# Decoder step on one core: the attention output's inverse norms made once a head instead of once per pair of query blocks

## The chip, the cores and the metric

The kernel runs on one core of one Trainium2 chip. The metric is device microseconds (us) of one execution. Three runs of the kernel before gave 3199.22, 3204.20 and 3204.82 us.

## What is computed

One step of a hybrid decoder layer: a SwiGLU feed-forward half step, a mixer that adds differential attention and retention under two gates, a second feed-forward half step, and a final norm. There is a prompt of 1024 rows and a sample of 8 x 4 rows, so 1056 rows in all. The part that matters here is the differential attention of the prompt (8 heads, each with two score maps of depth 64 and one value of width 128) and what becomes of its output:

```python
s = jnp.einsum('bqhcd,bkhcd->bhcqk', qh, kh)           # two maps c per head
p = jax.nn.softmax(jnp.where(mask, s, NEG_INF), axis=-1)
a = p[:, :, 0] - lam * p[:, :, 1]
o_a = jnp.einsum('bhqk,bkhv->bqhv', a, v)
o_a = rms_norm(o_a, subln_g, SUBLN_EPS) * (1.0 - lam_init)
merged = jax.nn.sigmoid(ga) * o_a + jax.nn.sigmoid(gb) * o_r
x = x + gate2 * (merged @ w_out)
```

The norm is over the 128 values of a head, so each query row of each head has one inverse norm. Keys and values of the prompt are outputs too.

## The kernel before

**Layout.** Activations lie transposed: features on the 128 partitions, rows along the free dimension, in 3 row blocks of 352. A large matrix product is made in three matmuls from a high and a low part of both operands (`mm3`, L228 to L230; `split`, L172 to L179, makes the parts: ACT rounds the high one, DVE or POOL subtracts for the low one).

**Stages.** Feed-forward 1, then the mixer, then feed-forward 2 and the final norm. The stage of this text is the differential attention, about 1480 to 2190 us. Its loop (L1236 to L1244) runs over heads h = 0 to 7 and weaves two generators. The *main* one is the gates' half units of earlier heads (`gates`, L1198) and then the projections of q, k and v of head h+1 (`qkv`, 18 steps); a step is 12 matmuls of 128x352. The *side* one is `attention(h)` (L1082). `weave` takes side steps at the ratio `DST`/(main steps), with `DST` = 52 (L888). So the order of the work is what these generators yield, and the instructions of each engine then run in the order in which they were recorded and scheduled, each waiting by semaphore for what it needs.

**attention(h).** The setup scales and splits q and k (`st`, `kk`, `kl`), turns k and v back into rows by transposes on PE (`kt` L1108, `vt` L1115, two halves of 512 rows each), copies each half from PSUM to SBUF on ACT (`ko` L1110, `vo` L1117; ring `kvo` of `KVO` = 4 buffers, L887) and stores it on POOL's queue (L1111, L1118), and splits v (`vh`, `vl`). Then, in five rounds, `scores(sb)` for the pair sb of query blocks (L1123) stands beside `values(sb-1)` (L1154). `scores` makes both maps of each block (PSUM `s`, L1133, two large buffers in all), mask and maximum on DVE (`mx` L1137), the exponential with row sums on ACT (`P` L1139), the norm's softmax term `l` (L1144) and the combination of both maps on DVE (L1149). `values` transposes the combined maps (`at`, L1163), splits them (`ah`, `al`) and multiplies with the values into `o`.

**The norm at the end of `values`.** ACT squares `o` (`osq` L1175) and copies it with the gain into `on`. Then `rsqrt_g` (L340): two matmuls with a column of ones sum the squares over the partitions (`rqo`, L347), so that each query row has its sum on a partition of its own; `rsqrt_cols` (L315) makes the inverse square root of [128, 2] on DVE by three Newton steps (L323 to L337, column by column for up to two columns); DVE multiplies the identity by each column (`rdo`, L359); after `RY` = 3 empty yields two matmuls ones x diagonal (L364) spread the inverse norms over all partitions. DVE multiplies `on` by them (L1180) and POOL's queue stores 128 KB to `od` in memory (L1181). This happens 4 times a head, 32 times in all.

**gates(h)** (L1198) makes the two gates of a head in row blocks, first g = 0 (the attention's, reads `od` back, L1213, and writes `M`, L1215) and then g = 1 (the retention's, reads `rd` and `ud`, adds to `M` on POOL and stores it to `md`). The gates of head 7 run later, beside w_out.

Of the kernel before, what the change touches and what calls it, by code (L numbers as in the profile page):

```python
# [11 lines left out]
F32 = mybir.dt.float32  # L12
# [3 lines left out]
ALU = mybir.AluOpType  # L16
# [4 lines left out]
P = 128  # L21
D = 1024
KT = 8
SEQ = 1024
# [4 lines left out]
NRB = 3  # L29
# [74 lines left out]
def build(tc, i):  # L104
    nc = tc.nc
    V, S, T, G = nc.vector, nc.scalar, nc.tensor, nc.gpsimd
    ld = nc.sync.dma_start
    st = nc.gpsimd.dma_start
# [29 lines left out]
    def aux_ps(name):  # L138
        return banks[0][1].tile([P, 512], F32, tag="aux", name=name, bufs=banks[0][3])
# [5 lines left out]
    od = [dr.tile([P, SEQ], F32, name=f"od{k}") for k in range(KT)]  # L145
    rd = [dr.tile([P, SEQ], F32, name=f"rd{k}") for k in range(KT)]
# [23 lines left out]
    def acth(out, in_, scale=1.0):  # L170
        if isinstance(scale, float):
            S.activation(out, in_, AF.Copy, scale=scale)  # L172
        else:
            S.activation(out, in_, AF.Identity, scale=scale)
# [97 lines left out]
    with tc.tile_pool(name="init", bufs=1) as ip:  # L272
        vec = ip.tile([P, P], F32, name="vec")
        o = 0
# [40 lines left out]
    def rsqrt_cols(sums, scale, eps, name):  # L315

        m, n = sums.shape
        x, h, a, y = (rsq.tile([P, 4], F32, tag=f"r{c}", name=f"r{c}{name}", bufs=2)[:m, :n] for c in "xhay")
        yi = y.bitcast(I32)
        if isinstance(eps, float):  # L320
            V.tensor_scalar(out=x, in0=sums, scalar1=scale, scalar2=eps, op0=ALU.mult, op1=ALU.add)
        else:
            V.scalar_tensor_tensor(out=x, in0=sums, scalar=scale, in1=eps, op0=ALU.mult, op1=ALU.add)  # L323
# [16 lines left out]

    def rsqrt_g(src, n, scale, eps, name):


        p_ = aux_ps(f"rq{name}")
        blocks = [(c, min(P, n - c)) for c in range(0, n, P)]
        for j, (c, w_) in enumerate(blocks):
            T.matmul(p_[:w_, 500 + j:501 + j], src[:, c:c + w_], ones[:, 0:1], start=True, stop=True)  # L347
        nb, w0 = len(blocks), blocks[-1][1]
        full = nb if w0 == P else nb - 1
        r = []  # L350
        for m, a, b in ((P, 0, full), (w0, full, nb)):
            if b > a:
                e = eps if isinstance(eps, float) else eps[:m, a:b]
                y = rsqrt_cols(p_[:m, 500 + a:500 + b], scale, e, f"{name}_{a}")
                r += [y[:, j:j + 1] for j in range(b - a)]
        dg = []
        for j, (c, w_) in enumerate(blocks):
            d = rsq.tile([P, P], F32, tag="rd", name=f"rd{name}_{j}", bufs=3)
            V.tensor_scalar(out=d[:w_, :w_], in0=ident[:w_, :w_], scalar1=r[j], scalar2=None, op0=ALU.mult)  # L359
            dg.append(d)  # L360
        for _ in range(RY):
            yield
        for j, (c, w_) in enumerate(blocks):
            T.matmul(p_[:, c:c + w_], ones[:w_, :], dg[j][:w_, :w_], start=True, stop=True)  # L364
        return p_
# [521 lines left out]
    KVO = 4  # L887
# [154 lines left out]
    with ExitStack() as left, ExitStack() as right:  # L1042
# [38 lines left out]

        def attention(h):  # L1082
# [40 lines left out]
            def scores(sb, A):  # L1123
                for qb in (2 * sb, 2 * sb + 1):
# [19 lines left out]
                    V.scalar_tensor_tensor(out=l2[sb][:, q:q + 1], in0=rs[:, 0:1], scalar=1e-5, in1=rs[:, 0:1],  # L1144
# [9 lines left out]
            def values(sb, A):  # L1154
# [21 lines left out]
                on = dp.tile([P, 256], F32, tag="on", name=f"on{h}_{sb}", bufs=2)  # L1176
                acth(on[:], po[:, :256], subg[:])
                yield
                rr = yield from rsqrt_g(sq[:], 256, 1.0 / P, l2[sb][:], f"o{h}_{sb}")
                V.tensor_tensor(out=on[:], in0=on[:], in1=rr[:, :256], op=ALU.mult)  # L1180
                st(out=od[h][:, sb * 256:(sb + 1) * 256], in_=on[:])  # L1181

            A = [[] for _ in range(4)]
            l2 = [dp.tile([P, 2], F32, tag="l2", name=f"l2_{h}_{sb}", bufs=4) for sb in range(4)]
            for sb in range(5):
                two = [scores(sb, A[sb])] if sb < 4 else []
                if sb:
                    two.append(values(sb - 1, A[sb - 1]))
                while two:
                    for g in list(two):  # L1190
                        try:
                            next(g)
                        except StopIteration:
                            two.remove(g)
                            continue
                        yield

        def gates(h):  # L1198
            M = gp.tile([P, SEQ], F32, tag="M", name=f"M{h}")
            ws = {}  # L1200
            for g, rb in ([(g, rb) for g in range(2) for rb in range(NRB)] if h < 7 else
                          [(g, rb) for rb in range(NRB) for g in range(2)]):
# [9 lines left out]
                ov = gp.tile([P, RB], F32, tag="gv", name=f"gv{h}_{g}{rb}", bufs=2)  # L1212
                (st if h == 7 else ld)(out=ov[:, :n], in_=(od, rd)[g][h][:, rc])  # L1213
                if g == 0:
                    V.scalar_tensor_tensor(out=M[:, rc], in0=t[:, :n], scalar=1.0, in1=ov[:, :n], op0=ALU.add, op1=ALU.mult)  # L1215
                    if n < RB:
                        V.tensor_scalar(out=gas[:, h, :], in0=t[:, n:], scalar1=1.0, scalar2=None, op0=ALU.add)
                else:
# [3 lines left out]
                    V.scalar_tensor_tensor(out=ov[:, :n], in0=t[:, :n], scalar=1.0, in1=ov[:, :n], op0=ALU.add, op1=ALU.mult)  # L1222
                    G.tensor_tensor(out=M[:, rc], in0=M[:, rc], in1=ov[:, :n], op=ALU.add)
                    st(out=md[h // 2][h % 2 * P:(h % 2 + 1) * P, rc], in_=M[:, rc])
# [182 lines left out]
```

## Time and profile before

| what | value |
|---|---|
| median of 3 runs | 3204.2 us (3199.22 to 3204.82) |
| the profiled execution | 3204.28 us, span 3202.5 us |
| TensorE matmul (PE) busy | 3060.3 us, 96% of the span |
| VectorE (DVE) busy | 1700.5 us, 53% |
| ScalarE (ACT) busy | 1151.3 us, 36% |
| GpSimd (POOL) busy | 452.0 us, 14% |
| granted TensorE clock, mean | 0.986 |
| memory traffic | 254.18 MB, 79 GB/s |

The span runs from the first to the last instruction; 1.8 us of the execution lie around it. PE is the matmuls and PEld the weight loads, which overlap them. Busy times are shares of the whole span and say nothing of one stage; a matmul's end is modelled, so PE's records overlap a little. In the rows, a name is that of a tile in the program without its buffer number, L is a line of the kernel printed above, and "idle before <- X" is how long the engine had stood idle ahead of an instruction and whose work ended that.

### The profile page before, as it was taken

The page shows a single profiled execution, that of the slowest core. Times are in us where ns is not written, and L with a number is a line of the kernel's source. Part 1 is how long each engine was busy: PE and PEld are TensorE (multiplying, and loading weights), DVE is VectorE, ACT ScalarE, POOL GpSimd, SP SyncE. Part 2 cuts the span into 40 slices and gives each one's busy share as a digit, 9 for nine tenths or more (in the row PEclk, how much of TensorE's full clock was granted, in tenths as well). Part 3 has the DMA queues.
Part 4 walks back from the last instruction along what each step waited for, and adds up shares of the span by engine and source line. Part 5 has one row for each costly group of instructions (what it writes and reads, how often), then busy time and mean ns, then how long its engine had stood idle before and what let it go on. Part 6 is the DMA issues. An engine that isn't in the chain of part 4 may idle for free.

```text
span 3202.5 us, 47920 instructions
## 1 busy us (share of the span) xinstructions
PE 3060.3 (96%) x19135; PEld 2925.4 (91%) x19135; DVE 1700.5 (53%) x3683; ACT 1151.3 (36%) x2164; POOL 452.0 (14%) x456
## 2 busy tenths in 40 slices
PE   7999999999999999999999998998999999999998
PEld 4999999999999999988888888988889999999998
DVE  6443434334366666668867777776655323233235
ACT  5422232222234243346555556554444111111113
POOL 2000000000132222212222222223021000000002
PEclk9999999999999999999999999998999999999999
DMA  6232222221131322222221121225622111111111
GB/s 215 61 116 81 80 91 87 86 79 53 52 121 59 100 77 83 89 84 84 75 65 60 56 71 56 73 68 172 202 74 66 47 46 47 47 47 47 47 47 61
DMA packets 261369, 254.18 MB, mean 79 GB/s; under 512 B 13216, under 2 KB 223649, under 8 KB 261146
## 3 DMA queue, kind: packets, MB, share of 16 engines
q1 hardware_dynamic: 245226, 200.38, 20.5%
q0 software_dynamic: 15920, 50.74, 4.5%
q8 instruction: 150, 2.46, 0.3%
q14 instruction: 73, 0.60, 0.1%
HBM read 207.56 MB, written 43.52 MB: 78 GB/s over the span
## 4 chain that ended last, share of the span: by engine, by line
PE 39%; DVE 9%; ACT 3%; issue 1%; DMA 1%; POOL 0%; DVEq 0%; SPq 0%; ACTq 0%; POOLq 0%
PE pb L228 3%; PE pa L228 3%; PE pa L229 3%; PE pa L230 3%; PE pb L229 3%; PE pb L230 3%; PE po L228 3%; PE po L229 2%; PE po L230 2%; PE gp L228 1%; PE gp L230 1%; PE gp L229 1%; ACT P L1139 1%; PE at L1163 1%; DVE rao L334 1%
## 5 line engine op out<-in xcount | busy, mean ns | idle before, releaser
L513 DVE TENSOR_TENSOR silu<-silu,pb 128x352 f32<-128x352 f32 x132 | 68.7, 521 | 503.5 <-PE pb L230 501.4
L172 ACT ACTIVATE gh<-silu 128x352 fp32r<-128x352 f32 x132 | 65.2, 494 | 325.4 <-DVE silu L513 325.2
L484 DVE SCALAR_TENSOR_TENSOR Y<-po,mod,Y 128x352 f32<-128x352 f32 (+1 forms) x144 | 82.1, 571 | 123.3 <-PE po L230 123.2
L447 POOL TENSOR_TENSOR acc<-acc,sq 128x352 f32<-128x352 f32 x27 | 29.8, 1103 | 804.7 <-ACT sq L446 795.8
L484 DVE SCALAR_TENSOR_TENSOR X<-po,mod,X 128x352 f32<-128x352 f32 (+1 forms) x144 | 81.7, 570 | 112.1 <-PE po L230 111.6
L512 ACT ACTIVATE silu<-pa 128x352 f32<-128x352 f32 x132 | 60.5, 458 | 205.9 <-PE pa L230 205.8
L1139 ACT ACTIVATE P<-s,mx 128x256 f32<-128x256 f32 (+7 forms) x128 | 94.9, 742 | 80.4 <-DVE mx L1137 72.2
L447 POOL TENSOR_TENSOR accf<-accf,sq 128x352 f32<-128x352 f32 x9 | 8.8, 974 | 726.8 <-ACT sq L446 726.8
L228 PE MATMUL po<-gh,wo_0h 128*128 128x352 f32 x288 | 94.6, 328 | 5.1 <-DVE X L484 4.1
L1137 DVE TENSOR_REDUCE mx<-s 128x1 f32<-128x256 f32 (+7 forms) x128 | 95.5, 752 | 1.8
L229 PE MATMUL po<-gl,wo_0h 128*128 128x352 f32 x288 | 93.8, 326 | 0.0
L230 PE MATMUL po<-gh,wo_0l 128*128 128x352 f32 x288 | 93.7, 325 | 0.0
L179 DVE TENSOR_TENSOR gl<-silu,gh 128x352 fp32r<-128x352 f32 x132 | 69.1, 524 | 46.2 <-ACT gh L172 45.8
L228 PE MATMUL po<-gh,wo_1h 128*128 128x352 f32 x288 | 93.4, 324 | 0.0
L230 PE MATMUL po<-gh,wo_1l 128*128 128x352 f32 x288 | 92.8, 322 | 0.0
L229 PE MATMUL po<-gl,wo_1h 128*128 128x352 f32 x288 | 92.6, 322 | 0.0
L172 ACT ACTIVATE ah<-at 128x512 fp32r<-128x512 f32 (+1 forms) x80 | 44.4, 555 | 98.4 <-PE at L1163 97.7
L228 PE MATMUL po<-gh,wo_3h 128*128 128x352 f32 x240 | 77.5, 323 | 1.2 <-DVE rs L489 1.2
L228 PE MATMUL po<-gh,wo_2h 128*128 128x352 f32 x240 | 77.7, 324 | 0.0
L229 PE MATMUL po<-gl,wo_2h 128*128 128x352 f32 x240 | 77.2, 322 | 0.0
L229 PE MATMUL po<-gl,wo_3h 128*128 128x352 f32 x240 | 77.2, 322 | 0.0
L230 PE MATMUL po<-gh,wo_2l 128*128 128x352 f32 x240 | 77.2, 321 | 0.0
(1511 smaller groups left out, 11358.7 us busy)
## 6 DMA issues: line engine op xcount, KB each, us to landing
ada_0r<-ada_w SPq DMA_DIRECT2D x18, 512.0 KB
ada_1r<-ada_w SPq DMA_DIRECT2D x18, 512.0 KB
ada_2r<-ada_w SPq DMA_DIRECT2D x18, 512.0 KB
ada_3r<-ada_w SPq DMA_DIRECT2D x18, 512.0 KB
st<-state_ret SPq DMA_DIRECT2D x32, 256.0 KB
state_ret_sample<-st POOLq DMA_DIRECT2D x32, 256.0 KB, 2.3
kp<-cache_k SPq DMA_DIRECT2D x64, 128.0 KB
vp<-cache_v SPq DMA_DIRECT2D x64, 128.0 KB
```

The costliest lines, as they stand in the source:

```text
L172: S.activation(out, in_, AF.Copy, scale=scale)
L179: (eng or V).tensor_tensor(out=l, in0=src, in1=f(h), op=ALU.subtract)
L228: T.matmul(out, wh, xh, start=first and j == 0, stop=False)
L229: T.matmul(out, wh, xl, start=False, stop=False)
L230: behind[0] = T.matmul(out, wl_, xh, start=False, stop=last and j == n - 1).ins
L334: V.scalar_tensor_tensor(out=a[:, j:j + 1], in0=y[:, j:j + 1], scalar=y[:, j:j + 1], in1=h[:, j:j + 1], op0=ALU.mult, op1=ALU.mult)
L447: (V if k % 2 else G).tensor_tensor(out=acc[k % 2], in0=acc[k % 2], in1=sq[:], op=ALU.add)
L484: V.scalar_tensor_tensor(out=x[k][:, c0:c0 + n], in0=p_[:, :n], scalar=gt[:, k, 0:1], in1=x[k][:, c0:c0 + n], op0=ALU.mult, op1=ALU.add)
L512: S.activation(s_[:], pa[:, :RB], AF.Silu)
L513: V.tensor_tensor(out=s_[:], in0=s_[:], in1=pb[:, :RB], op=ALU.mult)
L1137: V.tensor_reduce(out=mx[:], in_=ss[:, :wd], op=ALU.max, axis=AX.X, negate=True)
L1139: S.activation(pt[:, :wd], ss[:, :wd], AF.Exp, bias=mx[:], accum_out=rs[:, c:c + 1])
```

## The change

`rsqrt_g` goes. At the end of `values`, the two sums of a pair are added to the softmax terms in one tile `l2` of 8 columns (one DVE operation), and `on` becomes one tile of 128x1024 for the head (one buffer). A new generator `finish` makes one inverse square root of all 8 columns with `rsqrt_cols` (which for more than two columns goes by whole tiles), yields three times, and then, in two halves, makes four spread matmuls, one multiply of 128x512 and one store of 256 KB. A spread matmul now has the column itself, repeated 128 times, as its stationary operand, and the identity as the moving one; no diagonals are made. `finish` of head h is queued beside the first scores of head h+1 (`ends`); that of head 7 runs at its own end. In `gates` g = 1 now comes first and g = 0 second, and before g = 0 reads `od` it drains what is left of `finish`. `KVO` falls from 4 to 3, and the small tiles of `rsqrt_cols` grow from 4 to 8 columns.

```diff
     def rsqrt_cols(sums, scale, eps, name):
-        x, h, a, y = (rsq.tile([P, 4], F32, tag=f"r{c}", ..., bufs=2)[:m, :n] for c in "xhay")
+        x, h, a, y = (rsq.tile([P, 8], F32, tag=f"r{c}", ..., bufs=2)[:m, :n] for c in "xhay")
-        if isinstance(eps, float):
+        if scale is None:
+            x = sums
+        else:
             V.tensor_scalar(out=x, in0=sums, scalar1=scale, scalar2=eps, op0=ALU.mult, op1=ALU.add)
-        else:
-            V.scalar_tensor_tensor(out=x, in0=sums, scalar=scale, in1=eps, op0=ALU.mult, op1=ALU.add)
...
-    def rsqrt_g(src, n, scale, eps, name):
...
-    KVO = 4
+    KVO = 3
...
+        ends = {}
         def attention(h):
...
-                    V.scalar_tensor_tensor(out=l2[sb][:, q:q + 1], in0=rs[:, 0:1], scalar=1e-5, in1=rs[:, 0:1],
+                    V.scalar_tensor_tensor(out=l2[:, qb:qb + 1], in0=rs[:, 0:1], scalar=1e-5, in1=rs[:, 0:1],
...
-                on = dp.tile([P, 256], F32, tag="on", name=f"on{h}_{sb}", bufs=2)
-                acth(on[:], po[:, :256], subg[:])
+                acth(on[:, sb * 256:(sb + 1) * 256], po[:, :256], subg[:])
                 yield
-                rr = yield from rsqrt_g(sq[:], 256, 1.0 / P, l2[sb][:], f"o{h}_{sb}")
-                V.tensor_tensor(out=on[:], in0=on[:], in1=rr[:, :256], op=ALU.mult)
-                st(out=od[h][:, sb * 256:(sb + 1) * 256], in_=on[:])
+                pq = aux_ps(f"rq{h}_{sb}")
+                for j in range(2):
+                    T.matmul(pq[:, j:j + 1], sq[:, j * P:(j + 1) * P], ones[:, 0:1], start=True, stop=True)
+                V.scalar_tensor_tensor(out=l2[:, 2 * sb:2 * sb + 2], in0=pq[:, :2], scalar=1.0 / P,
+                                       in1=l2[:, 2 * sb:2 * sb + 2], op0=ALU.mult, op1=ALU.add)
+
+            def finish():
+                r = rsqrt_cols(l2[:], None, None, f"o{h}")
+                for _ in range(RY):
+                    yield
+                for hf in range(2):
+                    pr = aux_ps(f"rr{h}_{hf}")
+                    for j in range(4):
+                        T.matmul(pr[:, j * P:(j + 1) * P], r[:, 4 * hf + j:4 * hf + j + 1].to_broadcast([P, P]), ident[:],
+                                 start=True, stop=True)
+                    o_ = on[:, hf * 512:(hf + 1) * 512]
+                    V.tensor_tensor(out=o_, in0=o_, in1=pr[:], op=ALU.mult)
+                    st(out=od[h][:, hf * 512:(hf + 1) * 512], in_=o_)
+                    yield
...
-            l2 = [dp.tile([P, 2], F32, tag="l2", name=f"l2_{h}_{sb}", bufs=4) for sb in range(4)]
+            l2 = dp.tile([P, 8], F32, tag="l2", name=f"l2_{h}", bufs=2)
+            on = dp.tile([P, SEQ], F32, tag="on", name=f"on{h}")
             for sb in range(5):
                 two = [scores(sb, A[sb])] if sb < 4 else []
+                if sb == 0 and h:
+                    two.append(ends[h - 1])
...
+            ends[h] = finish()
+            if h == 7:
+                yield from ends[h]

         def gates(h):
...
-            for g, rb in ([(g, rb) for g in range(2) for rb in range(NRB)] if h < 7 else
-                          [(g, rb) for rb in range(NRB) for g in range(2)]):
+            for g, rb in ([(g, rb) for g in (1, 0) for rb in range(NRB)] if h < 7 else
+                          [(g, rb) for rb in range(NRB) for g in (1, 0)]):
...
+                if g == 0:
+                    for _ in ends[h]:
+                        pass
                 (st if h == 7 else ld)(out=ov[:, :n], in_=(od, rd)[g][h][:, rc])
                 if g == 0:
-                    V.scalar_tensor_tensor(out=M[:, rc], in0=t[:, :n], scalar=1.0, in1=ov[:, :n], op0=ALU.add, op1=ALU.mult)
+                    V.scalar_tensor_tensor(out=ov[:, :n], in0=t[:, :n], scalar=1.0, in1=ov[:, :n], op0=ALU.add, op1=ALU.mult)
+                    G.tensor_tensor(out=M[:, rc], in0=M[:, rc], in1=ov[:, :n], op=ALU.add)
+                    st(out=md[h // 2][h % 2 * P:(h % 2 + 1) * P, rc], in_=M[:, rc])
...
-                    V.scalar_tensor_tensor(out=ov[:, :n], in0=t[:, :n], scalar=1.0, in1=ov[:, :n], op0=ALU.add, op1=ALU.mult)
-                    G.tensor_tensor(out=M[:, rc], in0=M[:, rc], in1=ov[:, :n], op=ALU.add)
-                    st(out=md[h // 2][h % 2 * P:(h % 2 + 1) * P, rc], in_=M[:, rc])
+                    V.scalar_tensor_tensor(out=M[:, rc], in0=t[:, :n], scalar=1.0, in1=ov[:, :n], op0=ALU.add, op1=ALU.mult)
```

**Where the instructions now stand.** The rows below are instructions in the order of their engine; the line numbers of the changed kernel are 23 to 25 lower in this part.

DVE before, the end of head 1: the chain of its pair 2 (`rxo`, `ryo`, `rho`, `rao`), among the combination of the maps (`P`), the splits of head 2's keys (`kk`, `kl`) and the rotation of its queries (`q2t`).

```order
L323 SCALAR_TENSOR_TENSOR rxo_2_0_15196<-rqo_2_15193,l_1_2_14508 128x2
L1147 SCALAR_TENSOR_TENSOR rs_7_15104<-rs_7_15104,nlam 128x1
L324 TENSOR_SCALAR ryo_2_0_15199<-rxo_2_0_15196 128x2
L326 TENSOR_SCALAR rho_2_0_15197<-rxo_2_0_15196 128x2
L1149 SCALAR_TENSOR_TENSOR P_70_15113<-P_71_15158,rs_7_15104,P_70_15113 128x1024
L325 TENSOR_SCALAR ryo_2_0_15199<-ryo_2_0_15199 128x2
L1101 COPY ks<-dak 128x32
L334 SCALAR_TENSOR_TENSOR rao_2_0_15198<-ryo_2_0_15199,rho_2_0_15197 128x1 x2
L337 SCALAR_TENSOR_TENSOR ryo_2_0_15199<-rao_2_0_15198,ryo_2_0_15199 128x1
L1097 CAST kk_2_15494<-kk_2_15494 64x1024
```

DVE of the changed kernel, the end of head 1: the sum of the last pair, the chain on all 8 columns (its other two Newton rounds follow in the same manner), then head 2.

```order
L179 TENSOR_TENSOR al_33_15126<-at_33_15121,ah_33_15125 128x384
L1158 SCALAR_TENSOR_TENSOR l_1_14392<-rq_3_15151,l_1_14392 128x2
L325 TENSOR_SCALAR ryo_15407<-l_1_14392 128x8
L327 TENSOR_SCALAR rho_15405<-l_1_14392 128x8
L326 TENSOR_SCALAR ryo_15407<-ryo_15407 128x8
L330 TENSOR_TENSOR rao_15406<-ryo_15407 128x8
L331 TENSOR_TENSOR rao_15406<-rao_15406,rho_15405 128x8
L332 SCALAR_TENSOR_TENSOR ryo_15407<-rao_15406,ryo_15407 128x8
```

The chain moved from the middle of each round to the head's end, once, and nothing stands between its links.

PE before, the spread of that pair 2 of head 1, among the projection of head 2's queries (`q2p`).

```order
L229 MATMUL q2p_15241<-hl_119,q2h 128x352
L230 MATMUL q2p_15241<-hh_111,q2l 128x352
L228 MATMUL q2p_15241<-hh_112,q2h 128x352
L229 MATMUL q2p_15241<-hl_120,q2h 128x352
L364 MATMUL rqo_2_15193<-rdo_2_0_15216,ones 128x128
L364 MATMUL rqo_2_15193<-rdo_2_1_15218,ones 128x128
L230 MATMUL q2p_15241<-hh_112,q2l 128x352
L228 MATMUL q2p_15241<-hh_113,q2h 128x352
```

PE of the changed kernel, the first spread of head 1, among head 2's scores (`s`) and the gate of an earlier head (`gp`).

```order
L230 MATMUL gp_12_15474<-hh_109,g_1l 128x352
L1110 MATMUL s_11_15487<-kk_2_15297,st_2_15295 128x256
L1111 MATMUL s_11_15487<-kl_2_15299,st_2_15295 128x256
L1169 MATMUL rr_0_15499<-ident,ryo_15407 128x128 x4
L228 MATMUL gp_12_15474<-hh_110,g_1h 128x352
L229 MATMUL gp_12_15474<-hl_118,g_1h 128x352
```

The spread moved out of its own head into the next one, behind the second query block's scores; the second half (`rr_1`) follows 12 gate matmuls later.

ACT before, the setup of head 2, with the semaphores that each instruction waits for (DMASW is the landing of a store on POOL's queue).

```order
L1110 ACTIVATE ko_15519<-kt_15514 128x512 [waits DMASW5_49,PE_49]
L1117 ACTIVATE vo_15527<-vt_15522 128x512 [waits PE_49]
L1120 ACTIVATE vs<-dav 128x32 [waits Activation_49]
L172 ACTIVATE vh_15512<-vo_15527 128x512 [waits Activation_49]
L1110 ACTIVATE ko_15537<-kt_15532 128x512 [waits DMASW0_49,PE_49]
L1117 ACTIVATE vo_15545<-vt_15540 128x512 [waits DMASW1_49,PE_49]
L172 ACTIVATE vh_15512<-vo_15545 128x512 [waits Activation_49]
L1139 ACTIVATE P_00_15582,rs_0_15575<-s_00_15576,mx_00_15580 128x128 [waits DVE_49]
```

ACT of the changed kernel, the same place.

```order
L1087 ACTIVATE ko_15321<-kt_15316 128x512 [waits DMASW3_49,PE_49]
L1094 ACTIVATE vo_15329<-vt_15324 128x512 [waits DMASW4_49,PE_49]
L1097 ACTIVATE vs<-dav 128x32 [waits Activation_49]
L172 ACTIVATE vh_15314<-vo_15329 128x512 [waits Activation_49]
L1087 ACTIVATE ko_15339<-kt_15334 128x512 [waits DMASW5_49,PE_49]
L1094 ACTIVATE vo_15347<-vt_15342 128x512 [waits DMASW3_49,PE_49]
L1116 ACTIVATE P_00_15382,rs_0_15375<-s_00_15376,mx_00_15380 128x128 [waits DVE_49]
L172 ACTIVATE vh_15314<-vo_15347 128x512 [waits Activation_49]
```

With three buffers the fourth copy (`vo`, second half) takes the buffer of the same head's first `ko` and waits for that store; the first exponential now stands right behind it.

## Rows read from the trace of the kernel before

**Rows 1.** The page: span; then busy us (share of it) by engine.

```profile
span 3202.5 us, 47920 instructions
...
PE 3060.3 (96%) x19135; PEld 2925.4 (91%) x19135; DVE 1700.5 (53%) x3683; ACT 1151.3 (36%) x2164; POOL 452.0 (14%) x456
```

**Rows 2.** Stage window: length, PE/PEld/DVE/ACT/POOL busy, granted clock, DMA share, GB/s.

```profile
1480.00:2190.00 710.00, 652.30 (x4108) 611.33 (x4107) 535.66 (x1487) 388.92 (x783) 186.03 (x169) 0.98 0.22 68
```

**Rows 3.** Waits of PE in the stage: total us, times, longest.

```profile
PE rqo L364 <- DVE rdo L359: 37.0, 19, 3.3
PE at L1163 <- DVE P L1149: 7.4, 9, 1.2
```

**Rows 4.** Waits of PEld, the stage.

```profile
PEld rqo L364 <- DVE rdo L359: 44.1, 25, 3.6
```

**Rows 5.** PE timeline, head 1: start, length, instruction, idle before and releaser.

```profile
1641.18 0.32 PE L230 MATMUL v2p<-hh,v2l 128*128 128x352 f32 x1
1641.33 0.32 PE L228 MATMUL v2p<-hh,v2h 128*128 128x352 f32 x1
1643.43 0.71 PE L364 MATMUL rqo<-rdo,ones 128*128 128x128 f32 x4 [1.78 <-DVE rdo L359]
...
1645.00 0.49 PE L230 MATMUL v2p<-hh,v2l 128*128 128x352 f32 x1
1645.30 0.49 PE L228 MATMUL v2p<-hh,v2h 128*128 128x352 f32 x1
```

**Rows 6.** Two of the eight 6 us windows with half clock.

```profile
1642.00:1648.00 6.00, 4.57 (x20) 4.57 (x21) 1.96 (x5) 0.46 (x1) 0.56 (x1) 0.72 0.09 30
1717.00:1723.00 6.00, 3.81 (x17) 3.81 (x18) 5.69 (x15) 2.37 (x4) 0.56 (x1) 0.72 0.23 72
```

**Rows 7.** Waits of PE, 2100 to 2190 us, in head 7.

```profile
PE rqo L364 <- DVE rdo L359: 2.3, 2, 1.8
```

**Rows 8.** DVE groups by form, the final norm, 3100 to 3200 us.

```profile
L330 DVE TENSOR_TENSOR ray<-ray,rhy 128x4 f32<-128x4 f32 x3 | 0.5, 161 | 0.1
```

**Rows 9.** DVE groups by form, the stage: busy us, mean ns, idle before.

```profile
L334 DVE SCALAR_TENSOR_TENSOR rao<-ryo,rho 128x1 f32<-128x1 f32 x192 | 38.0, 235 | 0.5
...
L179 DVE TENSOR_TENSOR al<-at,ah 128x512 fp32r<-128x512 f32 x48 | 32.9, 686 | 19.4 <-ACT ah L172 19.4
L337 DVE SCALAR_TENSOR_TENSOR ryo<-rao,ryo 128x1 f32<-128x1 f32 x192 | 30.0, 164 | 0.5
...
L179 DVE TENSOR_TENSOR al<-at,ah 128x384 fp32r<-128x384 f32 x32 | 17.8, 555 | 15.8 <-ACT ah L172 15.4
...
L325 DVE TENSOR_SCALAR ryo<-ryo 128x2 int32<-128x2 int32 x32 | 16.9, 529 | 0.0
...
L359 DVE TENSOR_SCALAR rdo<-ident,ryo 128x128 f32<-128x128 f32 x64 | 15.2, 279 | 0.0
...
L1180 DVE TENSOR_TENSOR on<-on,rqo 128x256 f32<-128x256 f32 x32 | 13.3, 414 | 4.6 <-PE rqo L364 3.2 <-issue 0.7 <-ACT g_1h L172 0.7
```

**Rows 10.** Timeline of ACT, POOL and PE at the start of head 2.

```profile
1651.88 2.38 POOL L179 TENSOR_TENSOR g_1l<-g_1r,g_1h 128x1024 fp32r<-128x1024 f32 x1 [6.42 <-ACT g_1h L172]
...
1654.17 0.59 ACT L1117 ACTIVATE vo<-vt 128x512 f32<-128x512 f32 x1
1654.20 0.78 POOL L1111 DMA_DIRECT2D k_prompt<-ko  x1
...
1656.38 0.37 ACT L1139 ACTIVATE P<-s,mx 128x128 f32<-128x128 f32 x1 [0.96 <-DVE mx L1137]
...
1656.96 0.33 PE L1133 MATMUL s<-kk,st 128*128 128x256 f32 x1
```

**Rows 11.** Issue to landing of the 16 `ko` stores.

```profile
DMA to landing us min/median/max: 2.7/4.7/5.1
```

**Rows 12.** DMA issues: count, KB each, median us to landing.

```profile
od<-on POOLq DMA_DIRECT2D x32, 128.0 KB, 2.0
```

More of the change, by code (lines that the diff above doesn't have):

```diff
@@ L317, in rsqrt_cols @@
         m, n = sums.shape
-        x, h, a, y = (rsq.tile([P, 4], F32, tag=f"r{c}", name=f"r{c}{name}", bufs=2)[:m, :n] for c in "xhay")
+        x, h, a, y = (rsq.tile([P, 8], F32, tag=f"r{c}", name=f"r{c}{name}", bufs=2)[:m, :n] for c in "xhay")
         yi = y.bitcast(I32)
-        if isinstance(eps, float):
+        if scale is None:
+            x = sums
+        else:
             V.tensor_scalar(out=x, in0=sums, scalar1=scale, scalar2=eps, op0=ALU.mult, op1=ALU.add)
-        else:
-            V.scalar_tensor_tensor(out=x, in0=sums, scalar=scale, in1=eps, op0=ALU.mult, op1=ALU.add)
         V.tensor_scalar(out=yi, in0=x.bitcast(I32), scalar1=1, scalar2=None, op0=ALU.arith_shift_right)
@@ L339, in rsqrt_cols @@
         return y
-    def rsqrt_g(src, n, scale, eps, name):
[L344 to L365, printed above, removed]
     def rsqrt_s(src, n, scale, eps, name):
```

## The prediction

> **What bounds the kernel.** I read the page's busy shares first, then windows, then waits by engine, then timelines. TensorE is busy 96% of the span, DVE 53% [rows 1]. So DVE work that goes saves nothing by itself; what counts is where TensorE stands still for it. In the attention stage (1480 to 2190 us) PE is busy 652.3 of 710 us and DVE 535.7, three quarters [rows 2]: PE still bounds it, but with 57.7 us of gaps. The waits name them. The largest is the spread matmul L364 behind DVE's diagonals L359: 37.0 us in 19 waits, up to 3.3 us; the next, transposes behind the combined softmax L1149, is 7.4 us [rows 3]. The weight-load queue, which shows when the spread could have begun, has 44.1 us in 25 waits [rows 4]. The timeline shows a second price. The spread of head 1 came 1.78 us late; the projection matmuls ahead of it start 0.15 us apart, those behind it 0.30 us, the lower of TensorE's two levels (1.2 against 2.4 GHz) [rows 5]. A window of 6 us round it has a granted clock of 0.72 [rows 6]. There are eight such windows in the stage, each right behind a waited-for spread; not every late spread has one.
>
> **Why the spread is late.** Per pair of query blocks DVE makes 19 small operations in order: one that adds the softmax term, three that make the first guess, twelve Newton steps, two diagonals, the multiply. Only 8 to 36 matmuls stand between sums and spread on PE, since the three empty yields also count as side steps, and other DVE work (combine, rope, kk/kl splits) stands between the chain's links.
>
> **The change, part by part.**
>
> *A. The spread's wait goes, in heads 0 to 6.* The merged chain stands on DVE at the end of the head that it belongs to, the spreads on PE in the next head's first round. In head 2 that puts the last projections, the transposes of k and v and some 60 gate matmuls between last sums and first spread. 72 projection matmuls at 0.16 us (starts, [rows 5]) are 11.5 us alone, over three times the longest wait. So the waits fall to nothing: 37.0 us, plus about 0.16 us for each of the 19, because a matmul's record is 0.32 us long while the next starts 0.16 us on [rows 5], so that PE's idle time is undercounted: **-40**. Bounds 37.0 [rows 3] and 44.1 [rows 4].
>
> *B. The half clock goes with it.* 0.28 of 6 us is 1.68 us in each of eight windows [rows 6]: **-13.4**. If some have another cause, it is less.
>
> *C. Head 7 has no next head.* It runs its own finish at its end. Its price before, 2.3 us in two waits [rows 7], is inside A, so the new one must be added. Between its last sums and the first spread stand 16 matmuls, 2.6 us. DVE owes one add and twelve operations on eight columns. No row has eight columns; the nearest, 128x4, takes 0.161 us [rows 8], about what 128x1 takes (0.164, [rows 9]), so width is free there: 13 x 0.161 = 2.1 us. Two gate operations (at most the 0.555 us of a 128x384 one, [rows 9]) may stand between: 3.2 us in all, and handing over. **+1** (0 to 4).
>
> *D. KVO falls from 4 to 3.* Four copies a head (k, v, k, v) use the ring; the fourth must now wait for the store of the same head's first. At head 2 that store was issued at 1654.20, the fourth copy ran at 1654.17, the first exponential at 1656.38 [rows 10]. A store takes 4.7 us to land (2.7 to 5.1, [rows 11]): the copy would start at 1658.9, last 0.59 us, and the exponential behind it on ACT would be done near 1660.0. The score of the next query block, which needs that PSUM buffer back, stood at 1656.96 [rows 10]; the order now puts 12 more matmuls (1.9 us) ahead of it: 1658.9. Wait 1.1 us, times eight heads: **+9**. Between a store of 2.7 us (0) and of 5.1 (1.5 x 8 = 12). Behind ACT's wait also stand the second v split and the gate's tanh; their readers come later than that score.
>
> A page of the Trainium skill, "DMA: Bandwidth & Descriptors", section "Anatomy of one DMA — SWDGE (gpsimd) path", fits a store on this queue as 2.0 us plus bytes over 436e3, which for 256 KB is 2.6 us. By it D would be 0 and the sum 3152; the trace's median of 4.7 [rows 11] speaks against it, and I keep the trace.
>
> *E. One `on` tile, two large od stores.* The first `on` copy of a head waits for both od stores of the head before. From the second spread to that copy stand some 30 matmuls, 4.8 us; the multiply is 0.69 us (128x512, [rows 9]), a store of half the size 2.0 us [rows 12]. A weight split of 2.38 us [rows 10] can stand between on POOL; all four together are 5.1 plus the larger store. I take **0**, with 8 (1 us a head) as the bad end. The gate's od loads moved to second place in each head, behind a drained finish; they feed DVE and POOL, not PE, and M goes back to memory long before w_out reads it. The SP queue holds weight loads behind them; the stage moves 68 GB/s at a DMA share of 0.22 [rows 2], so I take 0.
>
> *F. DVE loses some 87 us off the path.* The five chain groups shown sum to 113.4 us [rows 9]; after, 8 x 12 x 0.161 = 15.5 and 16 multiplies at 0.686 = 11.0. PE's work hardly changes: eight sums and eight 128-wide spreads a head as before. Worth 0 where DVE is not waited for.
>
> **Sum.** -40 - 13.4 + 1 + 9 = -43.4. The profiled execution took 3204.28 us, the median of runs 3204.2, so the two are the same: **3161 us**. Best: -44.1 - 13.4 = 3147, rounded down to 3146. Worst of this case: -37.0 - 13.4 + 4 + 12 + 8 = -26.4, 3178, drawn in to 3175, since not all will be at their worst at once.
>
> **The rivals.**
>
> 1. *Half the gain: the waits move to the softmax.* Side steps per head fall from 42 to 35 of a budget of 52, so the same scores, transposes and splits come in fewer of PE's matmuls, about 1.2 times as dense, while DVE was three quarters busy [rows 2]. Then L1163 behind L1149, 7.4 us now [rows 3], takes what L364 gives up. For it: those waits exist already. Against it: DVE loses 87 us. If they rise to some 28 us, +21: 3182 (3175 to 3192).
>
> 2. *No gain: the merged chain is itself waited for.* It starts only once the last pair is summed, and half the spreads need it that had their columns long before. If the scheduler's order did not hide it, each head would wait once for up to 3.3 us [rows 3] and lose 1.7 us of clock, 8 x 5 = 40, beside D's 9: -53.4 + 40 + 9 = 3200 (3198 to 3211). For it: head 7. Against it: the order in heads 0 to 6. The Trainium skill's "Perfetto Trace Analysis", section "Optimizing Scalar/DVE Operations", speaks for this rival: "If Scalar/Vector aren't saturated, but are causing bubbles on other engines, breaking up instructions may allow work to be completed sooner." That is the case here (DVE 535.7 of 710, bubbles at L364), and the change does the reverse of breaking up; no run yet shows which of the two holds.
>
> 3. *Slower: ACT stops at the head's start.* ACT works in order, so a copy that waits for a store stops exponentials, tanh and splits behind it. If the fourth copy waits its full 4.7 us on PE's path, the `on` copy 2.0 us [rows 12] more, and PE then runs 1.7 us of half clock, that is 8.4 x 8 = 67: -53.4 + 67 + 1 = 3219. It decides from 53.4 / 8 = 6.7 us a head. For it: the store cannot leave before the POOL split ahead of it ends (1651.88 + 2.38, then 1654.20, [rows 10]). Against it: 12 matmuls more lie ahead of the score.
>
> **How the numbers follow.** Forecast 0.58, rival 1 0.22, rival 2 0.09, rival 3 0.11. About 0.2% (6.4 us) is what a measurement can tell from no change, so faster means below 3198: forecast, rival 1 and a sliver of rival 2, 0.81; same 0.09, from rival 2; slower 0.10, from rival 3. The range must leave out no more than 2 in 10: it takes the forecast and rival 1 nearly whole, 3146 to 3190, and leaves rivals 2 and 3.
>
> **What would show it.** Right: no PE wait at the spread except in head 7; no half-clock window behind one; PE's busy time in the stage the same, minus the clock's share; DVE near 450 us there; a wait of PE's third score behind ACT's exponential once a head, about 1 us. A is wrong if the spread still waits in heads 0 to 6; B if half-clock windows stay though the waits are gone; D if ACT's fourth copy starts with no idle time or if PE idles several us there; F (rival 1) if L1163 waits grow past 20 us. The prediction as a whole is wrong if the stage is not some 35 to 55 us shorter or if another stage changes length.

## The result and the profile after

| kernel | median of runs | ratio to before, 95% interval |
|---|---|---|
| before | 3202.8 us (3199.2 to 3204.8, 4 runs) | 1 |
| changed | 3180.6 us (3175.6 to 3181.7, 4 runs) | 0.9929 [0.9912, 0.9946] |

The change takes 22 us off. That is inside the range (3146 to 3190), but 20 us above the 3161 of the forecast and outside the forecast's own bounds (3146 to 3175). The page of the changed kernel's profiled execution (3181.72 us), against [rows 1]:

```profile
span 3180.0 us, 47390 instructions
...
PE 3052.8 (96%) x19135; PEld 2915.0 (92%) x19135; DVE 1649.4 (52%) x3219; ACT 1148.7 (36%) x2164; POOL 439.7 (14%) x440
```

TensorE has the same 19135 matmuls and is 7.5 us less busy, DVE 51 us. To compare the stage I take it from the first k transpose of head 0 to the first matmul of the part behind head 7's finish, since its end has moved: 1481.11 to 2183.24 us before, 1480.46 to 2162.80 after. The window after, with the columns of [rows 2]:

```profile
1480.46:2162.80 682.34, 640.73 (x4069) 599.87 (x4068) 475.31 (x996) 383.89 (x774) 167.28 (x146) 0.99 0.22 68
```

702.1 us have become 682.3. The rest of the 22.5 us by which the two profiled spans differ lies in 0.7 us ahead of the stage and 2 us behind it. PE's waits in this window, with the columns of [rows 3]:

```profile
PE s L1110 <- ACT P L1116: 14.5, 11, 2.9
PE o L228 <- ACT ah L172: 7.8, 19, 0.7
PE rq L1157 <- ACT osq L1152: 5.3, 6, 1.0
PE o L229 <- DVE al L179: 4.4, 8, 2.0
PE at L1140 <- DVE P L1126: 3.9, 3, 1.3
...
PE rr L1169 <- DVE ryo L332: 1.0, 1, 1.0
```

The spread's 37.0 us have become 1.0, and that one wait is in head 7. At the top now stands a wait that was 0.5 us before: the score behind ACT's exponential. Eleven of these, 14.5 us; seven of them, 10.1 us, are at the start of heads 1 to 7. The start of head 2, beside [rows 10]:

```profile
1642.44 2.37 POOL L179 TENSOR_TENSOR g_0l<-g_0r,g_0h 128x1024 fp32r<-128x1024 f32 x1 [10.00 <-ACT g_0h L172]
...
1644.77 0.80 POOL L1088 DMA_DIRECT2D k_prompt<-ko  x1
...
1649.74 0.60 ACT L1094 ACTIVATE vo<-vt 128x512 f32<-128x512 f32 x1 [4.91 <-DMA k_prompt<-ko]
...
1650.74 0.39 PE L1110 MATMUL s<-kk,st 128*128 128x256 f32 x1 [1.10 <-ACT P L1116]
```

The first `ko` store leaves 2.33 us after the POOL split began. ACT then stood still for 4.91 us until it had landed, made the fourth copy, and PE's score behind it was 1.10 us late. The seven fourth copies waited 4.73 to 5.48 us each, 34.8 us of ACT. The half clock is not all gone either. Three stretches are left, each behind a wait of PE, and only the last of the three waits is one of the seven behind a fourth copy. The three matmuls that ended these waits, and the window round the last:

```profile
1936.26 0.58 PE L229 MATMUL o<-al,vh 128*128 128x256 f32 x1 [2.03 <-DVE al L179]
...
2027.02 0.51 PE L1110 MATMUL s<-kk,st 128*128 128x512 f32 x1 [1.84 <-ACT P L1116]
...
2098.39 0.39 PE L1110 MATMUL s<-kk,st 128*128 128x256 f32 x1 [2.88 <-ACT P L1116]
```

```profile
2098.00:2104.00 6.00, 5.61 (x28) 5.58 (x29) 4.18 (x14) 2.69 (x10) 2.25 (x3) 0.72 0.33 104
```

Summed over windows of 2 us as (1 - granted clock) x 2, half clock costs 13.6 us of the stage before and 6.8 us after.

The attention stage in one table (us; waits of PE by what stood late, from the same views). The columns from `kvo4` on are experiments, which are told of below under these labels:

| | before | changed | kvo4 | k4_own | k4_col2 | b_vdve |
|---|---|---|---|---|---|---|
| stage | 702.1 | 682.3 | 660.9 | 674.9 | 666.0 | 674.1 |
| PE busy | 646.2 | 640.7 | 632.3 | 637.9 | 634.1 | 635.9 |
| lost to half clock, inside PE busy | 13.6 | 6.8 | 0 | 0 | 0 | 3.4 |
| wait at the spread | 37.0 | 1.0 | 1.0 | 8.7 | 0 | 13.2 |
| score behind the exponential | 0.5 | 14.5 | 2.3 | 0.3 | 3.6 | 0.5 |
| value product `o` behind `ah`, `al` | 3.1 | 12.2 | 10.3 | 9.9 | 14.0 | 8.1 |
| transposes behind the softmax | 7.4 | 3.9 | 4.1 | 13.7 | 5.7 | 8.1 |

### The profile page after: what moved, and what is told of

Its sections match the earlier page's. It is cut to its first block, busy times and chain, and to the rows that moved or that the text cites. A ratio compares the mean times of both kernels' runs of the same rounds, so it can differ in the third digit from the quotient of the medians.

```text
span 3180.0 us, 47390 instructions
## 1 busy us (share of the span) xinstructions
PE 3052.8 (96%) x19135; PEld 2915.0 (92%) x19135; DVE 1649.4 (52%) x3219; ACT 1148.7 (36%) x2164; POOL 439.7 (14%) x440
## 4 chain that ended last, share of the span: by engine, by line
PE 38%; DVE 5%; issue 5%; ACT 4%; DMA 2%; POOL 1%; SPq 0%; DVEq 0%; POOLq 0%; ACTq 0%
PE pb L228 3%; PE pa L228 3%; PE pa L229 3%; PE pa L230 3%; PE pb L229 3%; PE pb L230 3%; PE po L228 3%; PE po L229 3%; PE po L230 2%; DMA k_prompt<-ko 1%; PE gp L228 1%; PE gp L229 1%; PE gp L230 1%; PE s L1110 1%; PE s L1111 1%
## 5 line engine op out<-in xcount | busy, mean ns | idle before, releaser
L1110 PE MATMUL s<-kk,st 128*128 128x512 f32 (+2 forms) x192 | 70.0, 365 | 14.5 <-ACT P L1116 14.5
```

Source lines behind the costliest of these rows:

```text
L1110: T.matmul(ss[:, a:e], s_[:, qc], k_[:, a:e], start=True, stop=False)
```

## The experiments

My theory after the result: the spread's wait went as forecast, and what was lacking is the stall of the fourth copy (D), dearer than its waits. The first rival: the steps have become too dense, so that waits would only move on (rival 1 of the prediction). A second question was which part of the change earns the gain: the merged chain, or the queueing in the next head.

**Four buffers again (kvo4).** The room that `on` took comes from one `gu` buffer.

```diff
-    KVO = 3
+    KVO = 4
-                    uv = gp.tile([P, RB], F32, tag="gu", name=f"gu{h}_{g}{rb}", bufs=2)
+                    uv = gp.tile([P, RB], F32, tag="gu", name=f"gu{h}_{g}{rb}", bufs=1)
```

> The changed kernel with four kvo buffers again (one gu buffer given up for the room). Theory: ACT's wait for the store of the same head's first ko (34.8 us in 7 in the changed kernel) ends, and with it PE's wait of 1.0 to 2.9 us at the score once a head (10 us in 7), so 10 to 14 us less than the changed kernel's 3181: 3167 to 3171. Rival, the steps are too dense and the waits only move on to the softmax and the value product: within 4 us of 3181, with more waits at L1140 and o.

Measured: 3161.6 us, 0.9888 [0.9870, 0.9905]. The stage's window, and PE's waits in it:

```profile
1480.65:2141.59 660.94, 632.28 (x4071) 593.55 (x4069) 475.17 (x996) 386.18 (x774) 167.28 (x145) 1.00 0.23 70
```

```profile
PE o L228 <- ACT ah L172: 7.8, 17, 0.6
...
PE at L1140 <- DVE P L1126: 4.1, 4, 1.3
PE o L229 <- DVE al L179: 2.5, 6, 1.5
PE s L1110 <- ACT P L1116: 2.3, 2, 2.0
...
PE rr L1169 <- DVE ryo L332: 1.0, 1, 1.0
```

The score's wait falls from 14.5 to 2.3 us and the half clock is gone altogether (granted clock 1.00). Between the profiled runs the stage is 21.4 us shorter: 12.2 at the score, 6.8 of clock, 1.9 at `o`. The rival falls: the waits did not move on. By the ratios the copy's stall had cost 0.41% or 13 us, by the medians 19, more than the 10 to 14 that I expected; the medians of before that belong to the two differ by 4 us, so the size is known to some 6 us. The profiled runs overstate it, as they are the slowest of the changed kernel (3181.72) and the fastest of kvo4 (3160.06).

**Three buffers in the kernel before (b_kvo3).** `KVO = 3` and nothing else.

> The kernel before with KVO = 3 and nothing else. Theory: the fourth copy waits for the store here too, and the score of the second query block stands 12 matmuls earlier, so PE waits some 3 us a head, seven heads: +21, and up to 12 more if TensorE falls to half clock behind each: 3224 to 3236. Rival, ACT's delay is taken up by slack: under +6, 3203 to 3209.

Measured: 3233.2 us, 1.0102 [1.0086, 1.0117], 33 us slower, as the theory had it. PE's waits in its stage:

```profile
PE rqo L364 <- DVE rdo L359: 36.8, 19, 3.3
PE s L1133 <- ACT P L1139: 19.6, 10, 3.4
```

The spread's wait is as it was; the score's is new. Six of its ten are 2.96 to 3.42 us, one a head from head 2 on, where the changed kernel with 12 more matmuls of cover has 0.95 to 2.88. Here the clock has its price too. Behind each of the six the granted clock falls to half, which costs 15.4 us together by the sum used above, and the stage loses 30.7 us to half clock where the kernel before lost 13.6.

**The k and v stores on another queue (kv_sp).** KVO stays 3; four stores a head are issued on SP's queue.

```diff
-                st(out=kout[hf * 512:(hf + 1) * 512, hc].rearrange(...), in_=ko[:])
+                ld(out=kout[hf * 512:(hf + 1) * 512, hc].rearrange(...), in_=ko[:])
```

> The changed kernel with KVO = 3 kept, but the k and v stores issued on SP's queue and not on POOL's. Theory, the fourth copy waits because the first store stands behind POOL's weight split (2.4 us) and then takes 4.7 us to land; on SP it leaves right after the copy and lands sooner, so ACT's wait falls from 4.7 to 5.5 us to under 2 and PE's wait at the score goes: 3160 to 3168. Rival, the stores hold up the weight loads behind them on SP, or land no sooner: 3176 to 3190.

Measured: 3165.7 us, 0.9885 [0.9869, 0.9901], the same as four buffers. The fourth copy of head 2:

```profile
1643.24 0.60 ACT L1094 ACTIVATE vo<-vt 128x512 f32<-128x512 f32 x1 [0.84 <-DMA k_prompt<-ko]
```

ACT waits 0.84 us instead of 4.91, and the score does not wait there at all; PE's waits at the score in the stage are two, neither at a fourth copy:

```profile
PE s L1110 <- ACT P L1116: 2.3, 2, 2.0
```

So it is the store's way to memory, not the number of buffers as such, that PE had waited for; and the lost `gu` buffer of kvo4 does not explain its gain.

**Less dense steps (dst43).** `DST` = 43 for 52 in the changed kernel.

> The changed kernel with DST = 43 for 52, so that the 35 side steps of a head are spread over as much of the main work as the 42 were before (43/35 = 52/42). Theory that the steps are too dense: the added waits of PE at o (9.4 us more than before) and behind the exponential outside the head's start (4.4 us) go, and the score at the head's start comes later too: 3165 to 3173. Rival, density costs nothing: 3178 to 3184.

Measured: 3194.1 us, 0.9979 [0.9969, 0.9988], 14 us above the changed kernel. PE's waits:

```profile
PE o L229 <- DVE al L179: 13.0, 16, 2.2
PE o L228 <- ACT ah L172: 12.1, 19, 1.0
PE at L1140 <- DVE P L1126: 10.9, 9, 2.2
```

The theory that the steps are too dense falls, and so does the rival, that density costs nothing: with more main work between them, the waits at `o` double (12.2 to 25.1 us) and those at the transposes nearly treble (3.9 to 10.9). What sets them I take to be which main work and which ACT and DVE operations a step meets, but no run has tested it. **The other way (k4_dst60)**, `DST` = 60 on kvo4:

> As kvo4 (3162 us) with DST = 60 for 52. dst43 showed that spreading the side steps over more of the main work makes it slower (+13.5), since they then meet the rotation of the next head's queries on DVE. Theory, the other way round they meet it less: 3148 to 3158. Rival, 52 is the balance and denser steps lengthen the waits at the exponential, o and the transposes: 3164 to 3180.

Measured: 3164.3 us, 0.9875 [0.9860, 0.9890]: not to be told from kvo4's 0.9888. My guess about the rotation is not borne out.

**The finish at each head's own end**, both in the changed kernel (own_end) and on kvo4 (k4_own):

```diff
-                if sb == 0 and h:
-                    two.append(ends[h - 1])
...
-            ends[h] = finish()
-            if h == 7:
-                yield from ends[h]
+            ends[h] = ()
+            yield from finish()
```

> The changed kernel with the finish of every head at that head's own end, as for head 7, not in the next head. Theory: once the chain is merged and short (about 2.1 us), the 24 to 34 matmuls that still stand between the last sums and the spread cover it, so the queueing in the next head is worth little: 3176 to 3186. Rival, the queueing is what removed the waits: each head waits up to 3.3 us and loses up to 1.7 us of clock again, seven heads, +20 to +35: 3200 to 3215.

Measured: 3205.8 us, 1.0022 [1.0013, 1.0030]. My theory falls. The rival's range holds, but mostly by other waits than the spread's, which it named: against the changed kernel the spread has 7.8 us more, the transposes 9.6, the score 4.4 and half clock 5.1. PE's waits:

```profile
PE s L1110 <- ACT P L1116: 18.9, 10, 3.0
PE at L1140 <- DVE P L1126: 13.5, 13, 1.3
PE rr L1169 <- DVE ryo L332: 8.8, 8, 2.4
```

> As kvo4 (3162 us), but each head makes its finish at its own end. own_end stood 25 us above the changed kernel, with 8.8 us of waits at the spread, 9.6 us more at the transposes behind the softmax, 4.4 us more at the score and 5 us more of half clock. Theory, these are the price of the place and not of the copy's stall, so 15 to 28 us remain: 3177 to 3190. Rival, most of them came from the stall together with the place: under 8 us, 3160 to 3170.

Measured: 3176.8 us, 0.9924 [0.9910, 0.9937], 15 us above kvo4 by the medians and 12 by the ratios, just under what I expected. PE's waits:

```profile
PE at L1140 <- DVE P L1126: 13.7, 13, 1.3
PE rr L1169 <- DVE ryo L332: 8.7, 8, 2.4
```

Not queued, the spread waits in every head, and the transposes wait 13.7 us for 4.1. In five heads other DVE work (splits and rotation) stands ahead of the chain or among it, and the spread waits 0.60 to 0.62 us. The two long waits, 2.38 and 2.30 us, have another reason, to which the text comes back below: one operation of an otherwise unbroken chain lasts as long as an operation on POOL.

```profile
1552.01 2.35 POOL L179 TENSOR_TENSOR g_0l<-g_0r,g_0h 128x1024 fp32r<-128x1024 f32 x1 [18.84 <-ACT g_0h L172]
1552.04 2.33 DVE L330 TENSOR_TENSOR rao<-ryo 128x8 f32<-128x8 f32 x1
```

The queueing is worth these 12 to 15 us here; why the transposes wait longer without it was not traced.

**Per pair again, but queued (k4_col2).** On kvo4, the chain is made for two columns right behind each pair's sums (four times a head); spreads, multiply and store stay queued. (The tiles of `rsqrt_cols` get six buffers for two.)

```diff
+                Y.append(rsqrt_cols(l2[:, 2 * sb:2 * sb + 2], None, None, f"o{h}_{sb}"))
...
-                r = rsqrt_cols(l2[:], None, None, f"o{h}")
...
-                    T.matmul(..., r[:, 4 * hf + j:4 * hf + j + 1].to_broadcast([P, P]), ident[:], ...)
+                    T.matmul(..., Y[2 * hf + j // 2][:, j % 2:j % 2 + 1].to_broadcast([P, P]), ident[:], ...)
```

> As kvo4 (3162 us), but the inverse norms are made per pair again, on two columns right after that pair's sums, and only the spreads, the multiply and the store stay queued in the next head. Theory, the queueing takes the wait away and the saved DVE work is worth nothing: 3158 to 3168. Rival, DVE's load matters: some 45 us more of small operations in the middle of the rounds push the softmax, and PE's waits at L1140, o and the score grow by 10 us or more: 3172 to 3185.

Measured: 3166.0 us, 0.9888 [0.9872, 0.9903], the same ratio as kvo4. DVE is 25.8 us busier in the stage (501.0 for 475.2) and the ratio does not show it. PE's waits:

```profile
PE o L228 <- ACT ah L172: 9.9, 20, 0.9
...
PE at L1140 <- DVE P L1126: 5.7, 8, 1.4
PE o L229 <- DVE al L179: 4.1, 10, 1.5
PE s L1110 <- ACT P L1116: 3.6, 5, 1.6
```

The waits at `o`, the transposes and the score sum to 23.3 us for 16.7 in kvo4, and the profiled stage is 5.1 us longer, which is within the 6.3 us by which the four runs of kvo4 differ. The rival had 10 us or more. So merging the chain saves DVE work that costs nothing these times can tell.

**The gates in their old order (k4_g01)**, g = 0 first, on kvo4 (the `M` and `md` lines go back with it):

> As kvo4 (0.9888 of before), but the gates in their old order, g = 0 first: so the queued finish is drained before the first od load, the spreads stand some 20 matmuls earlier in the next head, and DVE's first gate operation waits for a store and a load of od just made. Theory, DVE and ACT work in order and stop there for several us a head behind the store's landing, so the reversal is a needed part of the change: 8 to 25 us above kvo4, a ratio of 0.991 to 0.997. Rival, the reversal is worth nothing: 0.987 to 0.990.

Measured: 3175.2 us, 0.9906 [0.9891, 0.9921]. The interval overlaps kvo4's, and the ratio lies just under the theory's, so the time alone doesn't settle it. The trace shows the mechanism at a part of its size: DVE waits 8.1 us in 5 for `gv` from `od`, and PE behind it at the transposes:

```profile
PE at L1140 <- DVE P L1126: 18.7, 13, 2.4
```

These were 4.1 us in 4 in kvo4.

**All that helped, together (k4_sp60)**, that is kvo4 with `DST` = 60 and the stores on SP:

> kvo4 with DST = 60 and the k and v stores on SP's queue, the three edits that helped or did no harm alone (0.9888, 0.9875, 0.9885). Theory, they share one cause, the copy's stall, which is gone already, and so do not add up: 0.986 to 0.989. Rival, each takes something of its own: below 0.985.

Measured: 3168.8 us, 0.9896 [0.9880, 0.9911], just above what I expected: they don't add up. kvo4 or kv_sp is the version to keep; both beat both kernels.

**Why the spread was late at all.** The trace of before showed something that I had not read. Around the longest spread wait, in order of time:

```profile
1711.83 3.00 POOL L179 TENSOR_TENSOR v3l<-v3r,v3h 128x1024 fp32r<-128x1024 f32 x1 [15.54 <-ACT v3h L172]
...
1712.50 2.36 DVE L325 TENSOR_SCALAR ryo<-ryo 128x2 int32<-128x2 int32 x1
...
1719.19 1.20 PE L364 MATMUL rqo<-rdo,ones 128*128 128x128 f32 x4 [3.27 <-DVE rdo L359]
```

A DVE operation on 128x2 numbers, 0.17 us elsewhere, lasts 2.36 us and ends with POOL's split of the v weights (1711.83 + 3.00 = 1714.83; 1712.50 + 2.36 = 1714.86). The same stands ahead of all five waits of 2.91 us or more. Three more operations of the chain are held like this for 2.27 to 2.35 us, two by v splits and one by a gate's, ahead of waits of 1.24, 1.89 and 2.07 us; the eight waits are 20.3 of the 37.0 us. Two edits of the kernel before; the first gives the v weights' split to DVE:

```diff
-            split(h[:], l[:], raw[:], eng=self.eng)
+            split(h[:], l[:], raw[:], eng=None if name[0] == "v" else self.eng)
```

> The kernel before with the low part of the v weights (128x1024, once a head) made by DVE and not by POOL. In the kernel before the five longest spread waits (2.91 to 3.27 us) each have a small DVE operation of the chain that lasts 2.35 to 2.37 us instead of 0.17 and ends when POOL's split of the v weights ends. Theory, the two engines do not run side by side there, so with the split on DVE itself, some 1.1 us, those operations last 0.17 us and the five waits shrink by about 1 us each, with less half clock: the L364 waits 37 to some 30 us, the time 5 to 12 us below before. Rival, the long records are late only on paper and DVE has more to do: waits at L364 the same or longer, the time 0 to 6 us above before.

Measured: 3171.2 us, 0.9908 [0.9893, 0.9923], 30 us faster, far more than expected:

```profile
PE rqo L364 <- DVE rdo L359: 13.2, 12, 1.9
```

From 37.0 to 13.2 us in 12 waits, none above 1.9, and half clock from 13.6 to 3.4 us; no chain operation is held for 2.3 us any more. DVE's own operation takes 1.21 us for POOL's 3.00. My sum had only the five long waits; seven waits went altogether. The spread's waits and the half clock are 34 us less in a stage that is 28 us shorter. POOL has 19 us less to do there as well (181.1 to 161.8 us), and whether that has a part in it was not tested apart. The second cuts the same POOL operation into eight of 128x128:

> The kernel before with the same POOL split cut into 8 operations of 128x128. Theory, a DVE operation that meets one is held only to the end of that piece, under 0.5 us: no chain operation of 2.3 us is left at the v splits, the five long waits come down by 1 to 2 us each and the half clock behind them goes: 5 to 16 us below before. Rival, POOL takes all its pieces before DVE gets its turn, or the pieces take longer in sum: waits and time as before or up to 5 us above.

Measured: 3200.1 us, 0.9992 [0.9982, 1.0002]. Pairs of the chain's operations that take 0.34 us elsewhere take 0.76 to 0.92 there, several in a row; the eight pieces take 4.46 us instead of 3.00, and the waits hardly change:

```profile
PE rqo L369 <- DVE rdo L364: 34.2, 19, 3.0
```

The theory holds for the length of one hold and fails for its sum. kvo4 and the v split on DVE together were not tried.

## Why the prediction was right or wrong

- **Direction and cause: right.** PE waited for the spread, and the change ended that: 37.0 us to 1.0. The three 0.16-us-a-wait microseconds that I added for overlapping records do not appear.
- **The size was not, and the range held by luck.** The change took half of what was forecast. 3180.6 us lies inside the range only because the range was drawn out for rival 1, whose mechanism did not come. By the sign that I set myself, a stage some 35 to 55 us shorter, the sum as a whole was wrong: the stage lost 19.8 us.
- **B was right in size, wrong in company.** "The half clock goes with it, -13.4": kvo4 shows exactly that, 13.6 us to none. In the changed kernel 6.8 us stayed, because other waits took the spread's place.
- **D is the step that failed, in its price.** Its wait was well foreseen: 1.1 us a head forecast, 0.95 to 2.88 measured, +9 over eight heads against 10.1 us over seven (head 0 has none). But D put nothing for what comes with such a wait, though I had just charged the old one for the half clock behind it. Without the copy's stall, in kvo4, the time is 13 to 19 us less, not 9. Directly behind the seven waits stands only 1.7 us of half clock, after the one of 2.88 us. The other 5.1 us of it, behind `o` and behind a later score, and some 4 us of waits at these places go with the stall too; by which way the stall made them is not shown. b_kvo3, with longer waits, has half clock behind every one. The rule that I set against the trace here, 2.6 us for a store of 256 KB (the Trainium skill, "DMA: Bandwidth & Descriptors", section "Anatomy of one DMA — SWDGE (gpsimd) path"), would have made D nothing; b_kvo3's 33 us speak against it.
- **The rest is small waits at `o`**, +9.1 us, which no step had. With -36.0 at the spread, -6.8 of clock, +14.0 at the score and -3.5 at the transposes they give -23.2; the stage lost 19.8. The other 3 us or so are in waits under 1 us each, 2.5 of them in five new waits of 0.5 us at the v projections.
- **C and E were right**: 1.0 us in head 7; one `on` copy of 32 waited, 0.77 us.
- **Rival 1 named the right time by the wrong way.** It gave 3182, but the transposes' waits fell, and in dst43 fewer side steps to the main work did not lower the waits.
- **Rival 2's rule** ("breaking up instructions may allow work to be completed sooner", the Trainium skill, "Perfetto Trace Analysis", section "Optimizing Scalar/DVE Operations") was neither borne out nor hurt: broken up or merged, the ratio is 0.9888.
- **F**: DVE's saving was worth nothing that a time here can tell, as said; its busy time fell by 53 us, not 87 (to 475, not 450), as back-to-back records overlap and six new ones are held by POOL (below).
- **"Why the spread is late"** was half the reason. I counted DVE's operations and not their lengths; a mean of 529 ns beside 164 for one as small [rows 9] was there to be asked about.

## What to carry to other kernels

Price a new wait on a nearly full TensorE not by its length alone but also by the half clock that may follow it, and look first at what a change gives away to make room: here one buffer less gave back a third to a half of the gain. Work that is late for TensorE was, here, better moved later in TensorE's order than made smaller. And when one of a series of equal small operations takes many times its usual length, see what the engine beside it was doing.

## What the hardware showed that I had not expected

Some small DVE operations that start while POOL runs a large one on SBUF last until POOL's ends. In the changed kernel, at the end of head 0, DVE and POOL in order of time:

```profile
1551.89 2.38 POOL L179 TENSOR_TENSOR g_0l<-g_0r,g_0h 128x1024 fp32r<-128x1024 f32 x1 [18.84 <-ACT g_0h L172]
1551.93 2.37 DVE L330 TENSOR_TENSOR rao<-ryo 128x8 f32<-128x8 f32 x1
```

0.17 us became 2.37, to 1554.30, with POOL's split ending at 1554.27; six of the 24 L330 records are like that. Not every operation is held. In head 1, under the v split:

```profile
1609.05 2.40 POOL L179 TENSOR_TENSOR v2l<-v2r,v2h 128x1024 fp32r<-128x1024 f32 x1 [12.24 <-ACT v2h L172]
1610.10 0.16 DVE L1123 RECIPROCAL rs<-rs 128x1 f32<-128x1 f32 x1 [1.54 <-ACT P L1116]
1610.30 1.17 DVE L1124 SCALAR_TENSOR_TENSOR rs<-rs,nlam 128x1 f32<-128x1 f32 x1
```

The reciprocal of one column passes in its usual 0.16 us; the operation behind it, with two inputs in SBUF, lasts to POOL's end. Operations that read PSUM pass too, such as `rxo<-rqo` (0.16 us, in the kernel before). It also goes the other way: POOL's v split takes 3.00 us in the five heads of the kernel before where DVE's combination L1149 (1.28 us) is still running when it begins, and 2.38 to 2.40 in the other three. The Trainium skill, "SBUF — State Buffer", section "SBUF: two separate sides", has the two engines share a pair of ports under an exclusive lock held for a whole instruction, taken by GpSimd's operations and by those of DVE that have two SBUF inputs or run in a mode with both ports. These rows agree, and b_vp8 shows holds that shorten with the piece (L325's counterpart 0.43 us for 2.36). L325 itself has one input, so it would have to be the mode's case; no row here shows the mode.

Second, stores of the same size on the same queue land at different times. In the changed kernel:

```profile
k_prompt<-ko POOLq DMA_DIRECT2D x16, 256.0 KB, 4.7
...
od<-on POOLq DMA_DIRECT2D x16, 256.0 KB, 2.6
```

Both are 256 KB, medians 4.7 and 2.6 us. The Trainium skill, "DMA: Bandwidth & Descriptors", section "Anatomy of one DMA — SWDGE (gpsimd) path", gives 2.6 for both. A row of `ko` is written in pieces of 128 numbers, one of `od` in pieces of 512, but that is not what makes the difference: stores of `vo`, in the same pieces, land in 2.71 to 2.73 us where they leave alone, as the fourth of heads 1, 3, 4 and 6 does after its stall. What the slow ones have in common is company. In the kernel before, the first `ko` stores of heads 1 and 2 took 2.73 and 4.82 us; the windows round them, with the columns of [rows 2]:

```profile
1560.40:1563.10 2.70, 2.70 (x22) 2.52 (x21) 2.67 (x16) 2.12 (x5) 1.84 (x3) 1.00 0.33 100
1654.20:1659.00 4.80, 4.80 (x33) 4.80 (x32) 3.40 (x10) 2.42 (x8) 3.02 (x5) 1.00 0.71 227
```

At head 2 a weight load of 512 KB (`q3r`) left on SP's queue 0.09 us after the store, and the DMA engines were twice as busy. No run moved that load by itself, so its share is not shown apart from that of the other k and v stores.
